# Sum of squared differences on one core: another assignment of row blocks to partitions

## The chip, the core and the metric

The kernel runs on one core of a Trainium2 chip. The metric is device time in microseconds: the median of three runs. A profile of one further execution gives the span from the first to the last instruction, which is somewhat shorter than the time. Engine names in the profile: DVE is VectorE, ACT is ScalarE, SP is the engine that issues the DMA transfers (SPq in the profile), POOL is GpSimd.

## The reference

Two arrays of 1024 rows of 4096 float32 are subtracted, squared and summed along each row:

```python
batch, dim = 1024, 4096
x, y: float32 (batch, dim);  axis = -1
def reference(x, y, axis):
    return np.sum((x - y) ** 2, axis=axis).astype(np.float32)
```

Both inputs together have 33.55 MB. The output has 1024 numbers.

## The kernel before

**Layout.** With 128 partitions, each partition takes 8 whole rows (R = 8, D = 4096), so N = R * D = 32768 columns of float32, 128 KiB for x and as much for y. Lines 61 to 63 give partition p the rows 8p to 8p+7, a contiguous block in DRAM:

```python
xv = x.rearrange("(p r) d -> p (r d)", p=P)
```

Whichever block a partition takes, nothing crosses partitions: each sums its own 8 rows into 8 columns of `results`.

**Buffers.** X and Y in SBUF hold H = 6 * D columns each, six of the eight rows. Column c of the input has its home at column c modulo H, so rows 6 and 7 take the place of rows 0 and 1.

**Loads.** The columns are cut into pieces: `xw` = 16384, 8192, 5568, 1824, 512, 288 for x, and `yw` = 16224, 8192, 2656, 2912, 928, 896, 512 for y, with two more of y at the end, of 288 and of 160 columns (the 160 are held back from the end of row 3). That makes 15 transfers, each over all 128 partitions, all issued by SP in one queue by `load` (line 108), each with a semaphore of its own. The first two are issued before the program's usual start (`prog.early`), two more right after it. These four fill the buffers. The other 11 go into columns that hold rows 0 and 1, so SP waits until ACT has squared row 0, then row 1.

**Arithmetic.** For each piece of y, DVE waits until it and the x that it needs have landed, and subtracts row by row in place (`sub`, line 165: X <- X - Y). ACT squares each difference and adds it up along the row (`square`, line 171, an activation with `accum_out`). Where a row comes in several pieces, the partial sums lie in `parts`, and DVE adds them (`complete`, line 178). The held-back piece of row 3 is squared on DVE (line 199). At the end SP stores `results` (line 226), 8 numbers per partition.

Of the kernel before, what the change touches and what calls it, by code (L numbers as in the profile page):

```python
# [48 lines left out]
def kernel(tc, x, y, axis, out):  # L49
    nc = tc.nc  # L50
    P = nc.NUM_PARTITIONS
# [5 lines left out]
    R = B // P  # L57
    N = R * D


    xv = x.rearrange("(p r) d -> p (r d)", p=P)
    yv = y.rearrange("(p r) d -> p (r d)", p=P)
    ov = out.rearrange("(p r) -> p r", p=P)


    H = 6 * D
# [31 lines left out]
    def home(c0, c1):  # L98
        h0 = c0 % H
        return slice(h0, h0 + c1 - c0)  # L100
# [4 lines left out]

    def load(landed, src, dst, name, c0, c1):
        sem = prog.semaphore("%s%d" % (name, len(landed)))
        nc.sync.dma_start(out=dst[:, home(c0, c1)], in_=src[:, c0:c1]).then_inc(sem, 16)  # L108
        landed.append(((c0, c1), sem))

    order = []
# [8 lines left out]
    for _ in range(2):  # L120
        load(*todo.pop(0))
    prog.early(mybir.EngineType.SP)
    while todo and todo[0][5] <= H:
        load(*todo.pop(0))
# [3 lines left out]
    for c0, c1 in ys:  # L128
        while c0 < c1:
            e = min(c1, (c0 // D + 1) * D)  # L130
            row_parts[c0 // D].append((c0, e))
            c0 = e
# [53 lines left out]
    for j, (c0, c1) in enumerate(ys):  # L186
# [3 lines left out]
        while c0 < c1:  # L190
            e = min(c1, (c0 // D + 1) * D)
            pieces.append((c0, e))
            c0 = e
        for piece in pieces:
            sub(*piece)
            r = piece[0] // D
            if final:
                nc.vector.wait_ge(diffs, n["diffs"])
                nc.vector.tensor_tensor_reduce(  # L199
                    out=Y[:, home(*piece)],  # L200
                    in0=X[:, home(*piece)],
                    in1=X[:, home(*piece)],
                    scale=1.0,
                    scalar=parts_of(r, 1),
                    op0=mult,
                    op1=add,
                    accum_out=results[:, r : r + 1],
                ).then_inc(sums, 1)
                n["sums"] += 1
                continue  # L210
            square(*piece, where[piece])
            squared[piece] = n["acts"]
            if r in (0, 1):

                nc.sync.wait_ge(acts, n["acts"])  # L215
                while todo and todo[0][5] <= H + (r + 1) * D:
                    load(*todo.pop(0))
                if r == 1:
                    while todo:
                        load(*todo.pop(0))  # L220
# [42 lines left out]
```

## Time and profile before

| | before |
|---|---|
| time, median of 3 runs (lowest, highest) | 85.19 us (85.11, 85.19) |
| span of the profiled execution | 83.5 us |
| DVE busy, ACT busy | 36.3 us, 31.7 us |
| first piece of x and of y, issue to landing | 22.0 us, 40.7 us |
| store of the result, issue to landing | 1.4 us |

The profile is read as follows. A line of a group names the source line, engine, operation, and the shape written and read, then the count, busy us and mean ns of one, and behind the last bar the idle time of that engine just before, with what ended most of it. The chain of waits is followed back from the last instruction, at each step to what released it. A DMA line gives packets, bytes and the mean rate; the line of a queue gives packets, MB and the time that the packets took, as a share of 16 DMA engines over the stretch asked for. A packet here is one contiguous run, that is, one partition's row of one transfer.

### The profile page before, as it was taken

How to read it: one execution, taken by the hardware profiler on the slowest of the kernel's cores; microseconds unless marked ns; L12 is line 12 of the kernel's file. 1: busy time of each engine (PE TensorE's matmuls, PEld its weight loads, DVE VectorE, ACT ScalarE, POOL GpSimd, SP SyncE). 2: the span in 40 equal slices, each digit the busy share in tenths (PEclk: the TensorE clock that was granted, in tenths of full speed). 3: DMA queues.
4: the chain of work that ended last, by engine and by line, in shares of the span. 5: the costliest groups of instructions: out<-in, count | busy, mean ns of one | idle time of the engine just before them, and what ended most of it. 6: DMA issues, size and time to landing. Idle time of an engine off the chain costs nothing.

```text
span 83.5 us, 109 instructions
## 1 busy us (share of the span) xinstructions
DVE 36.3 (44%) x18; ACT 31.7 (38%) x27; POOL 0.2 (0%) x4
## 2 busy tenths in 40 slices
DVE  0000000000000000000299999999099995979980
ACT  0500000000000000000001979697970897989990
POOL 0000000000000000000000000000000000000000
DMA  9389999956999999589989998997999899999920
GB/s 471 157 377 502 502 502 502 471 251 283 497 497 497 497 497 404 218 373 497 439 377 439 487 439 345 487 487 330 423 437 437 378 443 427 423 407 410 394 66 2
DMA packets 2305, 33.56 MB, mean 402 GB/s; under 512 B 385, under 2 KB 769, under 8 KB 1409
## 3 DMA queue, kind: packets, MB, share of 16 engines
q1 hardware_dynamic: 2304, 33.56, 94.7%
q14 instruction: 1, 0.00, 0.0%
HBM read 33.55 MB, written 0.00 MB: 402 GB/s over the span
## 4 chain that ended last, share of the span: by engine, by line
DMA 68%; ACT 14%; DVE 14%; SPq 1%; issue 0%
DMA Y<-in_y_dram 68%; ACT X L171 14%; DVE X L165 14%; SPq L108 1%; DVE results L178 0%; SPq L215 0%
## 5 line engine op out<-in xcount | busy, mean ns | idle before, releaser
L165 DVE TENSOR_TENSOR X<-X,Y 128x4096 f32<-128x4096 f32 (+9 forms) x14 | 35.8, 2593 | 45.2 <-DMA Y<-in_y_dram 45.1
L171 ACT ACTIVATE X<-X 128x4096 f32<-128x4096 f32 (+8 forms) x13 | 29.7, 2287 | 48.0 <-DVE X L165 48.0
L171 ACT ACTIVATION_READ_ACCUMULATOR X<-X 128x1 f32 x13 | 2.4, 186 | 0.0
L171 ACT ACT_TABLE_LOAD x1 | 1.3, 1283 | 1.9 <-PEq L19 1.9
L178 DVE TENSOR_REDUCE results<-parts 128x1 f32<-128x2 f32 (+1 forms) x2 | 0.3, 152 | 0.2 <-ACT X L171 0.2
L199 DVE CUSTOM_DVE_ANT_0 Y<-X,parts 128x160 f32<-128x160 f32 x1 | 0.4, 385 | 0.0
L244 POOL MEMSET const-bfloat16-1.0<- 128x1 bf16 x1 | 0.1, 101 | 0.0
L244 POOL MEMSET const-uint8-127<- 128x1 uint8 x1 | 0.1, 101 | 0.0
L244 POOL MEMSET const-float32-0.0<- 128x1 f32 x1 | 0.1, 98 | 0.2 <-issue 0.2
L244 POOL MEMSET const-float32-1.0<- 128x1 f32 x1 | 0.1, 98 | 0.0
L199 DVE DVE_READ_ACCUMULATOR2_ANT results<- 128x1 f32 x1 | 0.1, 83 | 0.0
## 6 DMA issues: line engine op xcount, KB each, us to landing
Y<-in_y_dram SPq DMA_DIRECT2D x1, 8112.0 KB, 40.7
X<-in_x_dram SPq DMA_DIRECT2D x1, 4096.0 KB, 48.9
Y<-in_y_dram SPq DMA_DIRECT2D x1, 4096.0 KB, 58.3
X<-in_x_dram SPq DMA_DIRECT2D x1, 2784.0 KB, 13.4
Y<-in_y_dram SPq DMA_DIRECT2D x1, 1456.0 KB, 19.2
Y<-in_y_dram SPq DMA_DIRECT2D x1, 1328.0 KB, 16.2
X<-in_x_dram SPq DMA_DIRECT2D x1, 912.0 KB, 21.0
Y<-in_y_dram SPq DMA_DIRECT2D x1, 464.0 KB, 21.6
```

Source lines behind the costliest of these rows:

```text
L108: nc.sync.dma_start(out=dst[:, home(c0, c1)], in_=src[:, c0:c1]).then_inc(sem, 16)
L165: nc.vector.tensor_sub(out=a, in0=a, in1=Y[:, home(c0, c1)]).then_inc(diffs, 1)
L171: nc.scalar.activation(out=a, in_=a, func=Square, accum_out=acc).then_inc(acts, 1)
L178: nc.vector.tensor_reduce(out=results[:, r : r + 1], in_=parts_of(r, len(row_parts[r])), axis=mybir.AxisListType.X, op=add,).then_inc(sums, 1)
L199: nc.vector.tensor_tensor_reduce(out=Y[:, home(*piece)], in0=X[:, home(*piece)], in1=X[:, home(*piece)], scale=1.0, scalar=parts_of(r, 1), ...
L244: nc = _bacc.Bacc("TRN2", target_bir_lowering=False, num_devices=1)
```

## The change

Partition p = 8e + i, with e from 0 to 15 and i from 0 to 7, takes block 16i + e of the rows rather than block p. The intent: the 16 groups of 8 consecutive partitions then read from neighbouring blocks of 128 KiB, where groups lay 1 MiB apart before. Within a group, the blocks of successive partitions lie 16 blocks, or 2 MiB, apart. The DRAM side of each transfer gets three dimensions (e, i, column); the SBUF side keeps its 128 partitions. The output is viewed in the same way, so each sum goes to its row.

```diff
-    xv = x.rearrange("(p r) d -> p (r d)", p=P)
-    yv = y.rearrange("(p r) d -> p (r d)", p=P)
-    ov = out.rearrange("(p r) -> p r", p=P)
+    G = 8
+    xv = x.rearrange("(i e r) d -> e i (r d)", i=G, r=R)
+    yv = y.rearrange("(i e r) d -> e i (r d)", i=G, r=R)
+    ov = out.rearrange("(i e r) -> e i r", i=G, r=R)
...
-        nc.sync.dma_start(out=dst[:, home(c0, c1)], in_=src[:, c0:c1]).then_inc(sem, 16)
+        nc.sync.dma_start(out=dst[:, home(c0, c1)], in_=src[:, :, c0:c1]).then_inc(sem, 16)
```

## The prediction

> **What bounds the kernel now.** I read the chain of waits first, because it says which resource ended last at each moment. Then I read the DMA queue and the rate slices, to see whether that resource is idle or full, and then single stretches of DMA, to find its rate per row.
>
> The chain that ended last, in order of time (start us, us, what):
>
> ```profile
> 0.43 40.69 DMA Y<-in_y_dram
> 41.14 8.77 DVE X L165 x2
> 49.93 3.72 ACT X L171 x2
> 54.11 16.24 DMA Y<-in_y_dram
> 70.37 2.94 DVE X L165
> 73.33 8.28 ACT X L171 x14
> 81.64 0.16 DVE results L178
> ```
>
> The chain is loads first and a short end of arithmetic. The 8.77 and 3.72 us in the middle are not idle time of the DMA: four loads were issued before 2.8 us, and the next one has to wait for a buffer, but the queue still has data to move. The page's queue line and the two long stretches below show that:
>
> ```profile
> DMA packets 2305, 33.56 MB, mean 402 GB/s; under 512 B 385, under 2 KB 769, under 8 KB 1409
> q1 hardware_dynamic: 2304, 33.56, 94.7%
> ```
>
> The load queue fills 94.7% of 16 engines' span of 83.5 us, which is 79.1 us per engine. The last load has landed at 80.5 us (issue at 65.07 and 15.4 to landing). So the engines run from about 1.0 us to 80.5 us with nothing to speak of between, and the rest is the 1.0 us at the front and 3.0 us at the end (last subtraction, square, sum, store). The two stretches, 3.5 to 18 us and 41 to 60 us:
>
> ```profile
> DMA packets 96, 6.29 MB, mean 434 GB/s; under 512 B 0, under 2 KB 0, under 8 KB 0
> q1 hardware_dynamic: 96, 6.29, 100.1%
> ...
> DMA packets 282, 8.15 MB, mean 429 GB/s; under 512 B 29, under 2 KB 29, under 8 KB 29
> q1 hardware_dynamic: 282, 8.15, 99.6%
> ```
>
> In the first stretch 96 rows of 65,536 B take 100.1% of 16 x 14.5 us, so a row takes 2.42 us and one engine moves 27.1 GB/s. The packet records agree: nearly every row of that size has 2.418 us, whatever DVE and ACT do beside it. [...] Only the first row of each engine is longer, 2.8 to 3.5 us on 15 of 16; the sixteenth starts 1.0 us after the others. That fill, about 0.75 us, is all that a better order of addresses in DRAM could save.
>
> DVE and ACT are far from the bound, 44% and 38% busy:
>
> ```profile
> DVE 36.3 (44%) x18; ACT 31.7 (38%) x27; POOL 0.2 (0%) x4
> L165 DVE TENSOR_TENSOR X<-X,Y 128x4096 f32<-128x4096 f32 (+9 forms) x14 | 35.8, 2593 | 45.2 <-DMA Y<-in_y_dram 45.1
> ```
>
> [...]
>
> **The change part by part.** Arithmetic, buffers, semaphores, the order of loads and their sizes are untouched, and so are rows of 64 KiB and less: each partition still reads one contiguous run of its 128 KiB block. The 14 subtractions (35.8 us), the squares (29.7 us) and the reductions stay as they are. The store writes the same 32 B per partition; its 1.4 us may move by 0.1.
>
> SP: the source has one dimension more. An issue takes 0.33 to 0.48 us now where the queue is not full. I allow 0 to 0.1 us for each; only the first lies on the path, and for the others 10 us and more of queued data hide it. Value 0.05, both ends in the range.
>
> DRAM side: [...] If the first rows are slow because of where they lie, up to 0.75 us come back; if not, none. I take 0.
>
> SBUF side: here is the cost. The source's slowest dimension is now e, with 16 indices for 16 engines[...]. All engines start row 0 within 0.25 us but for one (packet records)[...]. A row of 64 KiB takes 4.8 us instead of 2.42. [...]
>
> The sum: engine work without the fill is 79.1 - 0.75 = 78.3 us; doubled, 156.7. The lead d saved in each of 2 x 15 half loads: 0.1 to 0.25 us from the start times, and I take 0.2, so 6.0; 150.7 remain. Data start at 1.0, fill 0.75: the last load lands at 152.4. The end was 3.0; since DVE and ACT have caught up by then, 2.8. Span 155.2; the measured time is 1.7 above the span (85.19 against 83.5): 156.9, so 157. Both ends of d: 160 with 0.1, 155 with 0.25. The slower loads open no other wait: x and y of the second pair of loads keep the queue full for another 38 us after y's first load has landed, while the buffers come free 13 us after it (41.1 to 53.7 in the chain).
>
> **Rivals.**
> Nothing changes: [...] For it speaks that all 128 partitions are still written[...]. 85.2 with 0.05 of issue.
> Faster: as above, and the first rows no longer wait. For it speaks that only first rows are long; against it, that the first load of y, as far from x as can be, shows no such row (packet records: 2.394 to 2.401 us for all 128 rows of 64,896 B). 0.2 to 0.75 us less: 84.4 to 85.0, about 84.8. This ends on the other side.
> Memory: [...]
> Part of the loss: [...] Anything between 90 and 150.
>
> **How the numbers follow.** Ports shared in step: 0.50, at 157 (154 to 161). Part of the loss, or memory: 0.14. No change in the rate: 0.36, of which faster by the fill 0.21, within 0.2% 0.08, slower by issue or by a little contention 0.07. Faster 0.21, same 0.08, slower 0.50 + 0.14 + 0.07 = 0.71. The range must reach both cases: from 84.7 (which leaves out about 0.1 of the faster) to 161 (0.05 above).
>
> **What would show it.** Right: rows of 65,536 B at 4.8 us in pairs, the DMA share near 100% while the rate is about 217 GB/s, the first load of y landing near 79 us, DVE and ACT with the same durations and more idle time before each on DMA. In small loads at the end[...], the rate recovers. Wrong: rows of 2.42 us and 434 GB/s in the stretch from 3.5 to 18 us; then only the first rows are to be compared. [...]

## The result: nearly twice the time

The changed kernel takes 164.93 us (163.76 to 166.37) against 85.16 us (85.11 to 85.19), over four executions each. The ratio, 1.932 with a 95% interval of 1.922 to 1.942, leaves out the execution of 166.37 us as a slow one. The forecast was slower, 157 us with a range up to 161; the time lies 3.9 us above the range.

The head of the page and the DMA queue after:

```profile
span 161.9 us, 109 instructions
DVE 36.4 (23%) x18; ACT 32.2 (20%) x27; POOL 0.2 (0%) x4
DMA packets 2304, 33.56 MB, mean 207 GB/s; under 512 B 384, under 2 KB 768, under 8 KB 1408
q1 hardware_dynamic: 2304, 33.56, 97.2%
```

Same instructions, same bytes, same rows, and DVE and ACT are busy for about as long as before (36.4 and 32.2 us, 36.3 and 31.7 before). The load queue is as full as before (97.2%), of a span twice as long: 157.4 us per engine where it was 79.1. The engines don't wait; each row takes longer. The stretch from 3.5 to 18 us says by how much:

```profile
DMA packets 48, 3.15 MB, mean 217 GB/s; under 512 B 0, under 2 KB 0, under 8 KB 0
q1 hardware_dynamic: 48, 3.15, 105.6%
```

Half the rows of before in the same stretch: 1.056 x 16 x 14.5 us / 48 = 5.10 us for a row of 65,536 B, where it was 2.42. (The share goes over 100% because a row counts where it starts.)

Some pieces of the chain of waits, in order of time; the rows of dots stand for pieces left out (start us, us, what):

```profile
0.00 43.10 DMA X<-in_x_dram
...
43.15 39.85 another core or an unknown queue
...
83.02 8.77 DVE X L167 x2
...
91.82 3.72 ACT X L173 x2
...
96.21 45.74 DMA Y<-in_y_dram
...
158.46 1.16 ACT X L173 x4
...
159.64 0.16 DVE results L180
```

There is one core, so the "unknown queue" is the wait for the first load of y, which lands at 83.0 us (the page has 82.3 us from its issue at 0.69). The arithmetic pieces are as long as before, 8.77 and 3.72 us. ACT's long run at the end (8.28 us) is gone: it has time to catch up between loads. The queue never ran empty: the first load that had to wait for a buffer was issued at 95.6 us, while the fourth of the loads already issued landed only at 122.7 us.

### The profile page after: what moved, and what is told of

Its sections match the earlier page's. It is cut to its first block, busy times and chain, and to the rows that moved or that the text cites. A ratio compares the mean times of both kernels' runs of the same rounds, so it can differ in the third digit from the quotient of the medians.

```text
span 161.9 us, 109 instructions
## 1 busy us (share of the span) xinstructions
DVE 36.4 (23%) x18; ACT 32.2 (20%) x27; POOL 0.2 (0%) x4
## 3 DMA queue, kind: packets, MB, share of 16 engines
q1 hardware_dynamic: 2304, 33.56, 97.2%
## 4 chain that ended last, share of the span: by engine, by line
DMA 55%; another core or an unknown queue 29%; DVE 11%; ACT 3%; SPq 0%; issue 0%; DVEq 0%
DMA Y<-in_y_dram 28%; DMA X<-in_x_dram 27%; DVE X L167 11%; ACT X L173 3%; SPq L110 0%; DVE results L180 0%; DVEq L163 0%; SPq L217 0%
## 6 DMA issues: line engine op xcount, KB each, us to landing
Y<-in_y_dram SPq DMA_DIRECT2D x1, 8112.0 KB, 82.3
```

## The experiments

Two theories. **Ports** is the author's assumption behind the forecast: with 16 slowest indices in the source ("the split" below), engines write at the same time, two by two, through one way into SBUF, the core's memory, a port. No record names a port, or the engine that carried a row; what the runs can show is how long a row takes with which partitions written beside it. **DRAM**: the new order of addresses is slow, by the jump of 2 MiB from one row of a group to the next or by the closeness of the streams.

**e1_g4: the order in DRAM without the 16-way split.**

```diff
-    G = 8
+    G = 4
```

> G = 4 instead of 8: partition 4e+i takes block 32i+e, so the slowest dimension of the source has 32 indices. The order in DRAM keeps what the change wanted (neighbouring partition groups read neighbouring blocks of 128 KiB) and the jump from one row of a group to the next grows from 2 to 4 MiB. Ports theory: one e is now a run of 4 partitions[...]: rows of 65,536 B in 2.42 us, 434 GB/s in the long loads, time 85.2 to 85.8 (the issue of a three-dimensional source costs 0.2 us more and starts the data 0.4 us later). DRAM theory (it is the long jump between the rows of one engine, or the closeness of the engines' streams): no better than the change, 160 us or more.

Measured: 86.12 us (85.92 to 86.43), ratio to before 1.0104 (1.0083 to 1.0125). The stretch from 3.5 to 18 us:

```profile
DMA packets 96, 6.29 MB, mean 434 GB/s; under 512 B 0, under 2 KB 0, under 8 KB 0
q1 hardware_dynamic: 96, 6.29, 100.2%
```

This is the rate of before, with groups of partitions on neighbouring blocks and a jump of 4 MiB within a group. So neither closeness nor a jump of 4 MiB costs any rate here, and the DRAM theory falls; the jump of 2 MiB itself was not run with this split, but the next run has the loss without it. 32 indices instead of 16 are enough for 434 GB/s: one e is now a run of 4 partitions. The 0.9 us that remain are taken up below.

**e2_rev: the 16-way split with DRAM as before.**

```diff
-    xv = x.rearrange("(i e r) d -> e i (r d)", i=G, r=R)
+    xv = x.rearrange("(e i r) d -> e i (r d)", i=G, r=R)[:, ::-1, :]
```

(y and the output alike.)

> Source of three dimensions with 16 slowest indices as in the change, but each group of 8 partitions takes its own 8 consecutive blocks as before, in reverse order: partition 8e+i takes block 8e+7-i. DRAM is read as before, groups 1 MiB apart, no jump of 2 MiB. Ports theory: the 16-way split is what counts, so rows of about 5.1 us and 160 to 167 us, as after. DRAM theory: rows of 2.42 us and about 85.5 us.

Measured: 164.86 us (164.51 to 165.29), ratio 1.934 (1.931 to 1.938): the time of the change. The stretch from 3.5 to 18 us:

```profile
DMA packets 48, 3.15 MB, mean 217 GB/s; under 512 B 0, under 2 KB 0, under 8 KB 0
q1 hardware_dynamic: 48, 3.15, 105.8%
```

Each group reads its old blocks, in reverse order, and still a row takes 5.1 us. With e1 this is the pair that decides: the loss goes with the split, not with the addresses.

**e4_ports: which partitions are written.** Loads of rows of 64 KiB, each awaited:

```python
a = load(A, rows[:, 0:W])
for dst, lo, hi in ((Bt, 0, 64), (S, 32, 96), (Bt, 64, 128), (S, 0, 4), (Bt, 0, 1)):
    nc.sync.wait_ge(a, 16)
    a = load(dst[lo:hi, :], rows[lo:hi, W : 2 * W])
```

> Six loads one after the other, each awaited before the next, of rows of 64 KiB from the blocks of before; no arithmetic, the output is a dummy reduction. 128 partitions, then partitions 0-63, 32-95, 64-127, 0-3, and partition 0 alone. Ports theory: rows of 2.42 us for all 128 (19.4 us for the load), about 5 us for 0-63 and for 64-127 (20 us each, though they are half the bytes), 2.42 for 32-95 (10 us), about 10 us for 0-3[...], 2.42 for partition 0 alone. If instead an engine has one rate whatever port it writes: 19.4, 9.7, 9.7, 9.7, 2.4, 2.4 us.

The DMA lines of the stretches that hold the loads onto partitions 0-63, 32-95 and 64-127 (24 to 46.2, 47 to 58.6, 59.5 to 81.4 us; 64 rows and 16 packets of 4 B for the semaphore in each):

```profile
DMA packets 80, 4.19 MB, mean 189 GB/s; under 512 B 16, under 2 KB 16, under 8 KB 16
q1 hardware_dynamic: 80, 4.19, 91.2%
...
DMA packets 80, 4.19 MB, mean 362 GB/s; under 512 B 16, under 2 KB 16, under 8 KB 16
q1 hardware_dynamic: 80, 4.19, 89.6%
...
DMA packets 80, 4.19 MB, mean 192 GB/s; under 512 B 16, under 2 KB 16, under 8 KB 16
q1 hardware_dynamic: 80, 4.19, 91.8%
```

The 64 rows take 0.912 x 16 x 22.2 / 64 = 5.06 us each, then 2.60, then 5.03. In the packet records (the trace has start, time and bytes of each packet) all rows but an engine's first have 5.12, 2.42 and 5.12 us. Number of rows, their size and their pitch in DRAM are the same; only the partitions differ, and with them which blocks are read. The three times are those that were expected of the ports theory; why 32-95 is the odd one out, these runs don't show. Onto partitions 0-3 the four rows, which started within 0.8 us of one another, took 6.8 to 8.8 us each, where about 10 had been expected. Partition 0 alone took 3.4 us, within the 2.8 to 3.5 us that most first rows take in the kernel before; I had expected 2.4.

**e7_spread: a pair beside rows that are alone.** The same, with 16 or 8 single partitions in steps of 4 or 8:

```python
for lo, hi, step in ((32, 96, 4), (36, 100, 4), (0, 128, 8), (16, 48, 4), (0, 1, 1)):
    n = (hi - lo) // step
    nc.sync.wait_ge(a, 16)
    a = load(S[lo:hi:step, :], rows[0:n, :])
```

> Loads one after the other, each awaited, no arithmetic, a dummy output. After one of 128 partitions: 16 partitions 32, 36 to 92[...]; 16 partitions 36, 40 to 96[...]; 16 partitions 0, 8 to 120[...]; 8 partitions 16, 20 to 44[...]; and partition 0 alone. Rows of 64 KiB, two per engine. Ports alone: 2.42 us for the first, in the second 2.42 for 14 engines and 5.1 for two, 5.1 for the third, 2.42 for the fourth and fifth. If a jam spreads: the second above 2.42 for many engines. If each engine has a port of its own and is slow at any other: the second and fourth near 5.

Second rows in the packet records: 2.42 us for all in the first; in the second, 2.42 for 14 of them and 5.14 for exactly two; 5.12 to 5.14 for all 16 in the third; 2.42 for the fourth. All of these loads read from the first 16 blocks at most, so here the blocks can't be the cause. The DMA lines of the second and third (22 to 33.4 and 34 to 46.1 us):

```profile
DMA packets 48, 2.10 MB, mean 184 GB/s; under 512 B 16, under 2 KB 16, under 8 KB 16
q1 hardware_dynamic: 48, 2.10, 51.8%
...
DMA packets 48, 2.10 MB, mean 173 GB/s; under 512 B 16, under 2 KB 16, under 8 KB 16
q1 hardware_dynamic: 48, 2.10, 82.0%
```

In the second the engines are busy for only 52% of the stretch, because 14 are done while two still have rows of 5.14 us. The first and the second read the same blocks and differ in one partition, 96 in place of 32: that made two rows slow and left 14 as they were. So what counts is which partitions are written at the same time. Two rows that slow each other move 2 x 65,536 B in 5.12 to 5.14 us, 25.5 to 25.6 GB/s, less than the 27.1 of one row alone. Such a row, a shared one below, costs 2.12 times a row alone, not 2.

The fifth load, of partition 0 alone, was expected at 2.42 us a row and didn't test that. Its one row of 128 KiB went out as 16 packets of 8,192 B side by side, and the records of all 16 end 0.7 us after the first start (55.13 to 55.80 us), but the load landed only at 60.26 us. Its DMA lines (53.7 to 60.4 us; the other 16 packets are for the semaphore):

```profile
q1 hardware_dynamic: 32, 0.13, 6.1%
...
S<-in_x_dram SPq DMA_DIRECT2D x1, 128.0 KB, 6.5
```

From first start to landing, 131,072 B in 5.13 us are 25.5 GB/s, as much as two shared rows move together. And the records of the small packets ended here 4.5 us before their load had landed.

**e3_lead and e6_lead4: pairs held apart.** The two loads of the change with small loads ahead, meant to give one of each two engines that slow each other a lead of four rows. Which engines these are was assumed, not shown. The code is condensed:

```python
# e3_lead: W = 4 * D
load(S[0:4, :], rows[0:4, 0:W]); load(S[4:16, :], rows[4:16, 0:W])
# e6_lead4: W = 2 * D, S of 8 * D columns
load(S[0:32:8, :], rows[0:4, :]); load(S[4:100:8, :], rows[4:16, :])
# both, then
load(A, xv[:, :, 0:W]); load(Bt, yv[:, :, 0:W])
```

> Only the first two loads of the changed kernel (x and y, 16384 columns each, same blocks, same partitions), with no subtraction or square; the output is a dummy reduction. Ahead of them two small loads of one 64 KiB row per engine: one onto 4 partitions[...], one onto 12[...]. [...] Ports theory: after 20 us the rows of 65,536 B take 2.42 us though the addresses are those of the change, and both loads are in DRAM-to-SBUF at 434 GB/s between about 22 and 40 us; all landed near 60 us. DRAM theory: rows of 5.1 us, landed at 85 to 100 us.

> Two loads with the addresses and the split of the change, 8192 columns each (rows of 32 KiB), no arithmetic, a dummy output. Ahead of them a load on 4 partitions (0, 8, 16, 24) and one on 12 (4, 12 to 92), of 128 KiB per partition, or 4 rows' worth. [...] Ports in step[...]: rows of 32,768 B close to 1.21 us instead of 2.5, all landed near 35 us. A split that is slow for another reason[...]: 2.5 us, landed near 50 us.

e3 missed: all had landed at 98.4 us. The loads ahead were slow themselves (6.9 to 9.0 us a row), the groups of rows came out some 3 to 5 us apart instead of 10, four rows at 2.42 us (as far as the records let groups be told), and between 25 and 85 us three rows in four took 4.9 to 5.14 us and the fourth 4.6 to 4.8, 5.00 us on average. In e6, where they came 4 to 5 us apart, the stretch from 22 to 37 us has 124 rows of 32 KiB:

```profile
DMA packets 140, 4.06 MB, mean 271 GB/s; under 512 B 16, under 2 KB 16, under 8 KB 16
q1 hardware_dynamic: 140, 4.06, 94.6%
```

0.946 x 16 x 15 us / 124 = 1.83 us a row, half way between 1.21 alone and 2.5 in the changed kernel; in the records about one row in four takes 1.2 us and the others 1.5 to 2.4. All had landed at 45.3 us, between the 35 and the 50 that were expected. So behind these loads the same addresses and the same split cost less, 1.83 us a row instead of 2.5, but more than in my picture, in which all rows would pass alone for the whole of the lead. In e3 the rows ahead took 6.9 to 9.0 us, while in e7 a pair at 5.14 us left 14 others at 2.42. How far such a slowing reaches stays open.

**e8_cut and e9_cut_before: many small loads.** To see whether each load saves a fixed amount, as the lead in the forecast would have it, all loads are cut to 1024 columns (the waits count 16 for each part; e9 has the same with the source of before):

```diff
-        nc.sync.dma_start(out=dst[:, home(c0, c1)], in_=src[:, :, c0:c1]).then_inc(sem, 16)
+        k, m = c0, 0
+        while k < c1:
+            w = min(1024, c1 - k)
+            nc.sync.dma_start(out=dst[:, home(k, k + w)], in_=src[:, :, k : k + w]).then_inc(sem, 16)
+            k, m = k + w, m + 1
...
```

> The changed kernel with every load cut into transfers of at most 1024 columns (4 KiB per partition), 69 instead of 15; everything else as it is. If two engines share a port in step but for a lead of 0.2 to 0.35 us, and the lead is saved in every half of every transfer, [...]a row costs 1.5 to 1.8 times its time instead of 2.1, the loads take 117 to 138 us and the kernel 124 to 146. If the loss has nothing to do with who stands on which port at one time (the addresses, the split as such): 164 to 170, as after.

> The control: the kernel before with the same cut. [...]a cut changes only the number of issues (0.4 us each, about 28 us of SP, hidden behind 79 us of loads) and the small cost per row: 85 to 88 us.

Measured: 144.98 us (ratio 1.695, 1.686 to 1.704) and 89.06 us (1.045, 1.043 to 1.047), the first at the upper end of what was expected, the second 1 us above it: the control's rows of 4 KiB take 160 ns (median), where 27.1 GB/s would give 151, and over 456 such rows on each engine that makes about 4 us. With the split of the change such a row takes 286 ns, 1.8 times as long as in the control, not 2.1. (The profiled execution of e8 took 150.2 us, longer than the other three, 143.5 to 145.0.) The same cut makes the kernel before slower by 3.9 us and the changed one faster by 20. That agrees with a fixed saving in each load, and not with slow addresses, for which 164 to 170 us had been expected. It isn't shown that the saving comes of a lead in time. In the last load of e7 the records ended 4.5 us before the data had landed, and how much of that kind is in the times here isn't shown either. e6 speaks for a lead, e3 against it: there, with groups 3 to 5 us apart, four rows took 4 x (5.12 - 5.00) = 0.5 us less than shared rows all through. No run here separates the two.

**e5_halves: the aim of the change without its third dimension.**

```diff
-    xv = x.rearrange("(p r) d -> p (r d)", p=P)
+    xv = x.rearrange("(h p r) d -> h p (r d)", h=2, p=P)
...
-        nc.sync.dma_start(out=dst[:, home(c0, c1)], in_=src[:, c0:c1]).then_inc(sem, 16)
+        nc.sync.dma_start(out=dst[:, home(c0, c1)], in_=src[c0 // h, :, c0 % h : c0 % h + c1 - c0]).then_inc(sem, 16)
```

(with h = N // 2; y and the output likewise.)

> The aim of the change, neighbouring blocks for neighbouring partitions, without a third dimension in the loads: rows are dealt in two halves, partition p takes rows 4p to 4p+3 and 512+4p to 512+4p+3. Every load lies in one half, so its source has 128 slowest indices, 64 KiB apart instead of 128. If only the split and the longer issue count: rows of 2.42 us, first data at 1.0 us, 85.2 to 85.6 (the store has runs of 16 B instead of 32 and may take the longer issue, 0.2 to 0.4 us). If closeness in DRAM helps or harms by itself: the first rows shorter than 2.8 to 3.5 us and up to 0.75 us gained, or rows longer than 2.42.

Measured: 85.47 us, ratio 1.0034 (1.0021 to 1.0047). The stretch from 3.5 to 18 us:

```profile
DMA packets 96, 6.29 MB, mean 434 GB/s; under 512 B 0, under 2 KB 0, under 8 KB 0
q1 hardware_dynamic: 96, 6.29, 100.1%
```

Rows take 2.42 us, the first ones 2.4 to 3.3 (2.4 to 3.5 before): they are 0.2 us shorter on average, in one profile each, and the last load lands at the same time, 80.4 us against 80.5. Neighbouring blocks bring nothing that counts even where they cost no split. Of the 0.3 us that the kernel is longer, the store shows 0.2: 1.6 us to landing instead of 1.4.

**What is left of e1.** The issues of the first load of x and the store's landing, from the timelines and the issue lists: before, then e1_g4.

```profile
0.00 0.38 SPq L108 DMA_DIRECT2D X<-in_x_dram  x1
out_dram<-results SPq DMA_DIRECT2D x1, 4.0 KB, 1.4
```

```profile
0.00 0.64 SPq L110 DMA_DIRECT2D X<-in_x_dram  x1
out_dram<-results SPq DMA_DIRECT2D x1, 4.0 KB, 1.8
```

The third dimension costs 0.26 us in this issue, and 0.17 to 0.26 in the first four. At the front, the first data come at 1.4 us instead of 1.0, and the last load lands at 80.8 instead of 80.5; at the end the store lands 0.4 us later after its issue. Together about 0.8 us, the difference of the two spans (84.3 and 83.5). No version here beats the kernel before.

## Why the prediction was right in kind and missed in its size

**The bound.** Right. Every load engine was full before (94.7% of the span), each row of 65,536 B at 2.42 us, and the rest of the kernel had room to spare; no other wait opened.

**The DRAM side, taken at 0.** Right: 2.42 us a row before, in e1 and in e5, with three orders of addresses. The gain of up to 0.75 us by the first rows didn't come either: in e5 the last load landed 0.04 us earlier than before. No loss by the distance of the rows shows in these loads: a jump of 4 MiB left them at 434 GB/s.

**The SBUF side.** Right in kind: a row of 65,536 B takes 5.10 us instead of 2.42. The loss comes with 16 slowest indices in the source and the addresses of before (e2, 164.86 us) and goes with 32 (e1, 86.12 us), and e4 and e7 have rows of just this length, 5.12 to 5.14 us, by the choice of partitions. That in the change itself one engine carries each e, and that two at a time share a way into SBUF, was the author's inference and isn't shown, since the records name neither.

**The sum is where it failed: two terms, of opposite sign.** "Doubled, 156.7" took it that two engines share the rate of one, which was assumed. The measured price is 2.12 (e4, e7): 78.3 x 2.12 = 166.0, or 9.3 us more. Why two shared rows move less than one alone stays open. "So 6.0" was the author's estimate of what a lead d of one engine over another saves, from the start times in the trace of before; that it is saved once in each of 30 half loads was assumed. The engines were busy for 157.3 us by the packet records, so 8.7 us were saved against that price, 0.29 us in a half load rather than 0.2. By size of row, the packet records have these times per engine, all rows of a size together (sizes of 11,648 and 3,584 B and below 640 left out; the fill of the first rows is in the 20.1 of before):

```
row, B     before us   after us   ratio
 65,536      20.10       40.46     2.01
 64,896      19.16       39.96     2.09
 32,768      19.45       39.78     2.05
 22,272       6.62       13.33     2.02
 10,624       3.19        6.08     1.91
  7,296       2.21        4.03     1.83
  3,712       1.16        1.90     1.63
  2,048       1.34        1.84     1.37
  1,152       0.82        0.94     1.15
    640       0.26        0.26     1.00
```

At 2.12 throughout (measured with rows of 64 KiB only), each load of rows of 3,584 B or more saved 0.55 to 0.75 us, the loads with the largest rows included, and the smaller ones 0.3 to 0.5. So the saving per load hardly depends on its size, as the prediction's term has it; only its share grows as loads get smaller, and the ratio falls. (For the smallest rows it may fall too far, if their records end before their data has landed, as in e7.) What makes it stays open, as said under e8.

Net, the rows came out 9.3 - 2.7 = 6.6 us longer than forecast (the 157.3 have the first rows' fill of 0.75 in them, which the forecast added apart; hence the 5.8 below). The price of sharing alone puts the time outside the range; it had been taken as exactly 2, with no other end.

**SP and the store.** The issue was taken at 0 to 0.1 us more, and is 0.2 to 0.3. The first data come 0.4 us later. The end was to shrink to 2.8 us and was 3.3 (158.6 to 161.9), as the store takes 0.4 us longer to land. From first data to last landing the forecast had 151.4 us (150.7 and a fill of 0.75), and 157.2 passed (1.4 to 158.6). The span thus grew from the forecast 155.2 to 161.9 us by 0.4 at the front, 5.8 in the loads and 0.5 at the end. The other executions of the changed kernel had spans of 163.0 to 164.5, 1 to 2.6 us above the profiled one, for which I have no cause.

**The rivals.** That nothing changes, or that it gets faster, is excluded. "Memory" is excluded by e1 and e2. "Part of the loss" gave at most 150; only the small loads are like it, where the ratio falls to 1.6 and less.

## What to carry to other kernels

When a view of DRAM is changed, look at the slowest dimension that the transfer now has, not only at the addresses: here 16 instead of 128 halved the rate (217 GB/s instead of 434), 32 did not (434), with rows of the same size. These loads, with rows of 65,536 B at 2.42 us on every engine, gained nothing from the other orders in DRAM that were run. The mean time of one row by size, before and after, tells whether rows got slower or engines idle. If fewer than 128 partitions are to be loaded, it matters which: 64 rows took 5.1 us each onto partitions 0-63 and 2.4 onto 32-95.

## What the runs showed beyond expectation

Two rows that slow each other move less together (25.5 to 25.6 GB/s) than one alone (27.1). A third dimension in the source lengthened the first issue from 0.38 to 0.64 us, and one in the store's destination its landing from 1.4 to 1.8 us. Most first rows from idle took 2.5 to 3.5 us instead of 2.4 with each order of blocks tried before, in e1 and in e5. Each load with rows of 3,584 B or more was 0.55 to 0.75 us cheaper than 2.12 times the time of before, an estimate from rows of 64 KiB, whatever its size. Groups of rows 3 to 5 us apart gave almost nothing in e3 (5.00 us a row where shared ones take 5.12), and groups 4 to 5 us apart about half of what was hoped for in e6 (1.83 us, between 2.5 and 1.21); why, these runs don't tell.
